# A Hyena, attention and PEER block on one core: 32 more tokens by gathering, five gather buffers, a rebuilt second normalization

## The chip, the cores and the metric

The kernel runs on one core of a Trainium2 chip. The metric is the device time of one execution in microseconds (us). Engines: TensorE (PE; PEld is its weight load), VectorE (DVE), ScalarE (ACT), GpSimd (POOL), SyncE (SP, which issues most transfers). TensorE's clock has two levels, 1.2 and 2.4 GHz; the mean granted clock of the profiled execution is 0.989 of the upper one.

## The reference, cut to what matters

512 tokens of 1024 numbers pass a token mixer (Hyena convolution and neighbourhood attention), then a PEER layer, which is what the change touches. Each token is normalized, and 8 heads pick 16 of 16384 experts each, so 128 picks a token. An expert is one row of U and one of V.

```python
def modulate(x, g, shift, scale):
    return rmsnorm(x, g) * (1.0 + scale) + shift
...
    q = (hf @ p['peer_w_q']).reshape(T, PEER_HEADS, 2, PEER_D_HALF)
    s = jnp.einsum('thpd,hpnd->thpn', q, p['peer_keys'])
    top_s, top_i = lax.top_k(s, PEER_TOPK)
    ...
    g = jax.nn.softmax(best_s, axis=-1)
        act = jax.nn.gelu(jnp.einsum('td,thkd->thk', xb, u_tab[ib]), approximate=False)
        return jnp.einsum('thk,thkd->td', gb * act, v_tab[ib])
        x_next = x_next + g2 * peer(modulate(x_next, p['norm2_g'], sh2, sc2), p)
```

## The kernel before

Products that need nearly full precision are made of halves: an operand is rounded to `h` (ScalarE, a copy into fp32r), the rest `l` is the difference (VectorE, sometimes GpSimd; `split`, line 205), and TensorE sums `h*h + h*l + l*h`.

The PEER layer treats the tokens in two ways. The first 128 take their rows by gathering: for each of the 128 picks, GpSimd issues an indirect transfer that brings one row of U (later of V) for each of 128 tokens into a tile `row` of 512 KB (line 1278, three buffers). VectorE makes the dot products with the normalized tokens `h2n` (line 1283), later the weighted sum of V rows (line 1292). This is the generator `sparse`, 256 steps, of which the calling loops take one or more at a time.

The other 384 tokens are dense. The 16384 experts are taken as 128 blocks i of 128. `low(i)` multiplies block i of U with the tokens: 24 matmuls of 384 columns (lines 233 and 235), whose gelu goes into a tile of the `ring` (51 buffers, line 1024). Which picks a token has is written as a dense matrix G: `spread` goes over 24 groups of 16 tokens, builds one-hot tiles on VectorE (`eq`, `gl`, `gh`, lines 1253 to 1258), multiplies them on TensorE (lines 1264 and 1265), evicts `st` on ScalarE and writes it to memory (`Gd`). G is read back for 8 blocks at a time (line 1076).

The V loop (line 1071) then does for each block i: `w` = ring * G on VectorE (line 1081); `wsh`, `wsl`, the halves of `w`; `vh`, `vl`, the halves of the block of V; and 18 matmuls of 512 columns into six accumulators, two for each 128 tokens (lines 223 to 225). As long as `low`s are left, one goes between two V products.

The stages in time: mixer to about 611 us; second normalization (`experts`, `modulate`, lines 423 to 435) with the two first query projections to 640; `route` (scores and top 16), with twelve `low`s between, to about 829; `columns` and `spread` with `low`s to 1028; V loop with 75 `low`s and then without them to 1891; the last output transfer ends the span.

The order on each engine is made by a scheduler when the program is built; the lines of code set its priorities, and `issue_after` holds an operation's transfers or gathers behind an instruction. Two buffers each hold `ws`, `v`, `wh`/`wl` (weight halves) and the PSUM tile of a `low`; three hold `raw` (weight blocks as loaded).

Of the kernel before, what the change touches and what calls it, by code (L numbers as in the profile page):

```python
# [34 lines left out]
NT = 3  # L35

RING = 51
# [132 lines left out]
class Kernel:  # L170
# [251 lines left out]
    def modulate(self, pool, h, xT, a, b, r, tap=None, bufs=2):  # L422
        nc = self.nc
        n = xT.shape[-1]
        for db in range(8):
            t = self.t(pool, "md", [128, n], bufs=bufs)
            nc.vector.tensor_tensor(t, r[db > 1] if isinstance(r, list) else r, xT[:, db, :], ALU.mult)
# [4 lines left out]
            last = self.split_into(h[0][:, db, :], h[1][:, db, :], t, "p" if db % 2 else "v")  # L432
            if tap is not None:
                tap(db, t)
        return last
# [357 lines left out]
    def run(self, st):  # L793
# [127 lines left out]
        with ExitStack() as s1:  # L921
# [38 lines left out]
            for tb in range(4):  # L960
# [10 lines left out]
                nc.sync.dma_start(xn[tb * 128:tb * 128 + 128, :], o)  # L971
            rb = self.t(self.pool(xst, "rb2", side="left"), "rb", [128, 512])
# [3 lines left out]
        self.sh2, self.a2 = sh2, a2  # L976
        self.experts(dr, [xst, yost, hst2, hst], x, xn, rb)
# [3 lines left out]
    def experts(self, dr, done, x, xn, r):  # L981

        nc, V = self.nc, self.nc.vector
        nd = NT * 128
# [4 lines left out]
        h2n = pl.tile([128, 1024], F32, name="h2n")  # L989
# [3 lines left out]
        with ExitStack() as s1:  # L993
            mp = self.pool(s1, "mod2", side="right")

            def tap(db, t):
                if db % 4 == 0:
                    nat.append(self.ps("s"))
                nc.tensor.transpose(nat[-1][:, (db % 4) * 128:(db % 4) * 128 + 128], t[:, 0:128], self.ident)
                if db % 4 == 3:  # L1000
                    nc.scalar.activation(h2n[:, (db - 3) * 128:(db + 1) * 128], nat[-1], AF.Copy)
            last = self.modulate(mp, h2, x, self.a2, self.sh2, r, tap, 4)
            with self.tc.issue_after(last[0]), self.tc.issue_after(last[1]):
                ks, row = self.tables(tp, mp)
# [30 lines left out]
        cols, rows, g0, mm = self.columns(cp, self.pool(s1, "picks", side="left"), pi, pj, pg, nd)  # L1035
# [4 lines left out]
        sparse = self.sparse(sp, h2n, rows, g0)  # L1040
# [9 lines left out]
        O = [[self.ps("s" if n < 4 else "t") for n in (2 * b, 2 * b + 1)] for b in range(NT)]  # L1050
# [10 lines left out]
        def finish(b, y, res):  # L1061

            o = self.t(sp, "row", [128, 1024], bufs=3)
            for hf in range(2):
                d = slice(hf * 512, hf * 512 + 512)
                V.tensor_tensor(o[:, d], y[hf], g2[:, d], ALU.mult)
                V.tensor_tensor(o[:, d], o[:, d], res[:, d], ALU.add)
            dst = self.A["out"].rearrange("(r q c) d -> q r c d", r=ROWS, q=QB)[b]
            nc.sync.dma_start(dst, o)

        for i in range(NE):
            while todo and todo[0] < i + RING:
                low(todo.pop(0))
            if i % 8 == 0:
                G = self.t(vp, "G", [128, nd // 16, 8, 16], bufs=2)
# [8 lines left out]
            if i < NE - 2:  # L1084
                products(i, range(NT))
            with self.tc.issue_after(ins):
                for _ in range((2 + i % 2) if todo else 1):
                    next(sparse, None)
            if i == NE - 8:
                g2 = self.load(self.wp, None, "wh", self.g2d, 2)  # L1090
                res = self.t(vp, "G", [128, 3, 1024], bufs=2)
                nc.sync.dma_start(res, xn[128:, :].rearrange("(b p) d -> p b d", p=128))
        r0 = self.t(self.wp, "wh", [128, 1024], F32, 2)
        nc.sync.dma_start(r0, xn[:128, :])
        for _ in sparse:
            pass
        finish(0, [self.acc[:, hf * 512:hf * 512 + 512] for hf in range(2)], r0)
        mm = products(NE - 2, [0])
        for b in range(3):
# [5 lines left out]
            finish(b + 1, O[b], res[:, b])  # L1105
        hs.close()

    def tables(self, tp, mp):
# [3 lines left out]
        row = self.load(tp, "sel", "row")  # L1112
        for g in range(4):
            s = slice(4 * g, 4 * g + 4)
            keys = self.load(mp, "keys", src=self.A["keys"][:, s], bufs=2)
            self.split_into(ks[0][:, s], ks[1][:, s], keys, "p" if g % 2 else "v")
        return ks, row

    def route(self, rp, h2, ks, row, pi, pj, pg, ahead):
# [3 lines left out]
        self.id16 = rp.tile([128, 128], F16, name="id16")  # L1123
        V.tensor_copy(self.id16, self.ident)
# [94 lines left out]
    def columns(self, cp, hp, pi, pj, pg, nd):  # L1219
# [3 lines left out]
        ei = cp.tile([128, 128], I32, name="ei")  # L1223
        V.scalar_tensor_tensor(ei, flat(pi), 128.0, flat(pj), op0=ALU.mult, op1=ALU.add)
        g0 = cp.tile([128, 128], F32, name="g0")
        V.tensor_copy(g0, flat(pg))
        hi = {}
        for n, x in (("i", pi), ("j", pj), ("g", pg)):
            p = self.ps("s", 128, nd)
            for b in range(NT):  # L1230
                mm = nc.tensor.transpose(p[:, b * 128:b * 128 + 128], x[:, 4 - NT + b].rearrange("p h k -> p (h k)"), self.ident).ins
            hi[n] = hp.tile([128, nd, 2], F16, name="p" + n)
            pp = p.unsqueeze(2).to_broadcast([128, nd, 2])
# [6 lines left out]
        return hi, ei, g0, mm  # L1240
# [29 lines left out]
    def sparse(self, vp, h2n, ei, g):  # L1270

        nc, V = self.nc, self.nc.vector
        dots = vp.tile([128, 128], F32, name="dots")
        acc = self.acc = h2n

        def gather(tab, n):
            r = self.t(vp, "row", [128, 1024], bufs=3)
# [3 lines left out]
        for n in range(128):  # L1281
            r = gather("u_rows", n)
# [27 lines left out]
```

## Time and profile before

| | us |
|---|---|
| median of 3 runs | 1901.79 (1900.74 to 1902.36) |
| profiled execution | 1902.87 |
| its span | 1901.1 |
| TensorE busy | 1817.8 (96%) |
| VectorE busy | 1470.5 (77%) |
| ScalarE busy | 836.3 (44%) |
| GpSimd busy | 566.9 (30%) |
| moved | 429.37 MB, mean 226 GB/s |

The busy share is a mean over stages with different limits. A stage's limit is seen in slices of the span, and within a slice in the timeline, where a row's bracket tells how long the engine sat idle ahead of it and who released it.

### The profile page before, as it was taken

What the parts mean: (1) busy time and instruction counts of PE and PEld (TensorE: products, weight loads), DVE (VectorE), ACT (ScalarE), POOL (GpSimd) and SP (SyncE); (2) the same over time, 40 slices, a digit from 0 to 9 for tenths busy, and PEclk for the clock granted to TensorE, in tenths of its full rate; (3) what the DMA queues carried; (4) which work ended last, traced back from release to release, by engine and by line L of the source; (5) the groups of instructions that cost most, each with busy time, mean ns of one, the idle gap of its engine ahead of it and who ended that gap; (6) DMA issues with size and microseconds to landing.
All of it is one profiled execution on the core that took longest, in us unless ns stands there. A gap on an engine that the chain in (4) does not pass through costs nothing.

```text
span 1901.1 us, 26935 instructions
## 1 busy us (share of the span) xinstructions
PE 1817.8 (96%) x9939; PEld 1566.5 (82%) x9939; DVE 1470.5 (77%) x2742; ACT 836.3 (44%) x1265; POOL 566.9 (30%) x381
## 2 busy tenths in 40 slices
PE   6999999999989899999999999999999999999997
PEld 1578887878867788899989898889999999988886
DVE  7879765656788788878997877778777777768875
ACT  2553434545552543346876333233333333333332
POOL 3440000000002433341221444444444444433410
PEclk9999999999999999999999999999999999999999
DMA  9453323333486322246888988889898888878873
GB/s 304 143 172 113 109 84 117 117 114 92 128 292 226 125 78 78 78 134 236 330 308 321 349 305 306 312 297 336 312 328 302 316 313 303 321 249 305 305 269 106
DMA packets 167389, 429.37 MB, mean 226 GB/s; under 512 B 14967, under 2 KB 70455, under 8 KB 163288
## 3 DMA queue, kind: packets, MB, share of 16 engines
q1 hardware_dynamic: 127112, 280.82, 43.9%
q0 software_dynamic: 40144, 146.82, 20.8%
q8 instruction: 78, 1.28, 0.3%
q14 instruction: 55, 0.45, 0.1%
HBM read 387.22 MB, written 38.27 MB: 224 GB/s over the span
## 4 chain that ended last, share of the span: by engine, by line
PE 73%; DVE 11%; issue 5%; POOL 3%; ACT 2%; DMA 1%; SPq 0%; ACTq 0%; DVEq 0%; POOLq 0%
PE a L233 26%; PE a L235 12%; PE s L223 7%; PE s L224 6%; PE s L225 6%; PE t L225 3%; PE t L224 3%; PE t L223 3%; POOL row L1278 3%; PE s L1264 1%; PE s L1265 1%; PE a L756 1%; DVE gh L1258 1%; DMA row<-in_u_rows,ei 1%; DVE sc L1155 1%
## 5 line engine op out<-in xcount | busy, mean ns | idle before, releaser
L233 PE MATMUL a<-h,wh 128*128 128x384 f32 (+1 forms) x2944 | 613.9, 358 | 6.2 <-ACT ring L1024 1.3
L233 PEld LDWEIGHTS a<-h,wh 128*128 128x128 f32 x2944 | 524.3, 189 | 53.8 <-DVE h L205 2.4
L204 ACT ACTIVATE wh<-raw 128x1024 fp32r<-128x1024 f32 (+1 forms) x208 | 213.7, 1027 | 358.5 <-DMA raw<-in_u_cols 162.9
L235 PE MATMUL a<-h,wl 128*128 128x384 f32 (+1 forms) x1472 | 318.4, 354 | 0.0
L1278 POOL DMA_INDIRECT row<-in_u_rows,ei x128 | 187.0, 1461 | 336.7 <-DVE row L1283 321.8
L1278 POOL DMA_INDIRECT row<-in_v_rows,ei x128 | 200.4, 1565 | 261.9 <-DVE h2n L1292 242.6
L235 PEld LDWEIGHTS a<-h,wl 128*128 128x128 f32 x1472 | 261.4, 188 | 17.4
L205 DVE TENSOR_TENSOR wl<-raw,wh 128x1024 fp32r<-128x1024 f32 (+1 forms) x173 | 203.8, 1178 | 60.5 <-ACT wh L204 40.0
L224 PE MATMUL s<-vl,wsh 128*128 128x512 f32 x512 | 200.0, 392 | 7.1 <-DVE vl L205 7.1
L1283 DVE SCALAR_TENSOR_TENSOR row<-row,h2n 128x1024 f32<-128x1024 f32 x128 | 155.0, 1220 | 57.0 <-DMA row<-in_u_rows,ei 56.8
L225 PE MATMUL s<-vh,wsl 128*128 128x512 f32 x512 | 198.3, 390 | 0.0
L204 ACT ACTIVATE wsh<-w 128x384 fp32r<-128x384 f32 x128 | 67.0, 524 | 287.8 <-PE t L224 137.9
L223 PE MATMUL s<-vh,wsh 128*128 128x512 f32 x512 | 176.2, 390 | 0.0
L1292 DVE SCALAR_TENSOR_TENSOR h2n<-row,dots,h2n 128x1024 f32<-128x1024 f32 x127 | 162.5, 1279 | 16.5 <-DMA row<-in_v_rows,ei 16.0
L205 DVE TENSOR_TENSOR vl<-raw,vh 128x1024 fp32r<-128x1024 f32 x128 | 155.8, 1218 | 5.9 <-ACT vh L204 5.8
L205 DVE TENSOR_TENSOR wsl<-w,wsh 128x384 fp32r<-128x384 f32 x128 | 71.1, 556 | 97.5 <-ACT wsh L204 81.9
L204 ACT ACTIVATE vh<-raw 128x1024 fp32r<-128x1024 f32 x128 | 134.5, 1051 | 26.1 <-DMA raw<-in_v_rows 23.3
L446 POOL DMA_DIRECT2D yv<-in_w_ada x32 | 17.2, 537 | 380.7 <-DVE yv L456 165.2
L205 POOL TENSOR_TENSOR wl<-raw,wh 128x1024 fp32r<-128x1024 f32 x35 | 85.0, 2428 | 125.4 <-PE a L235 106.8
L224 PEld LDWEIGHTS s<-vl,wsh 128*128 128x128 f32 x512 | 96.3, 188 | 26.8 <-DVE vl L205 9.8
L225 PEld LDWEIGHTS s<-vh,wsl 128*128 128x128 f32 x512 | 96.4, 188 | 19.9
L223 PEld LDWEIGHTS s<-vh,wsh 128*128 128x128 f32 x512 | 96.1, 188 | 17.5 <-ACT vh L204 0.5
(357 smaller groups left out, 2978.1 us busy)
## 6 DMA issues: line engine op xcount, KB each, us to landing
raw<-in_u_cols SPq DMA_DIRECT2D x128, 512.0 KB, 3.7
raw<-in_v_rows SPq DMA_DIRECT2D x128, 512.0 KB, 3.7
Gd<-st SPq DMA_DIRECT2D x24, 1024.0 KB, 5.3
G<-Gd SPq DMA_DIRECT2D x16, 1536.0 KB, 11.9
raw<-in_w_in SPq DMA_DIRECT2D x40, 512.0 KB, 3.9
yv<-in_w_ada POOLq DMA_DIRECT2D x32, 256.0 KB
adaw<-in_w_ada SPq DMA_DIRECT2D x16, 512.0 KB, 5.6
raw<-in_w_q SPq DMA_DIRECT2D x16, 512.0 KB, 3.4
```

Of the source, the lines that this page charges most:

```text
L204: return (nc.scalar.activation(hi, src, AF.Copy).ins, (nc.vector if eng == "v" else nc.gpsimd).tensor_tensor(lo, src, hi, ALU.subtract).ins)
L205: (nc.vector if eng == "v" else nc.gpsimd).tensor_tensor(lo, src, hi, ALU.subtract).ins)
L223: t.matmul(out, a[0], b[0], start=start, stop=False)
L224: t.matmul(out, a[0], b[1], start=False, stop=False)
L225: return t.matmul(out, a[1], b[0], start=False, stop=stop).ins
L233: t.matmul(out, w[0][:, c, :], h[x][:, c, :], start=(c == 0 and x == 0), stop=False)
L235: i = t.matmul(out, w[1][:, c, :], h[0][:, c, :], start=False, stop=(c == n - 1))
L756: nc.tensor.matmul(po[:, e], a, vv[:, tb, e], start=(n == 0), stop=False, skip_group_check=True)
L1155: V.match_replace(s, v[:, 0:8], s, -3.0e38)
L1278: nc.gpsimd.indirect_dma_start(out=r, out_offset=None, in_=self.A[tab], in_offset=bass.IndirectOffsetOnAxis(ap=ei[:, n:n + 1], axis=0))
L1283: V.scalar_tensor_tensor(r, r, 1.0, h2n, op0=ALU.mult, op1=ALU.mult, accum_out=dots[:, n:n + 1])
L1292: V.scalar_tensor_tensor(acc, r, dots[:, n:n + 1], acc, op0=ALU.mult, op1=ALU.add)
```

## The change

32 more tokens (`NX`) go by gathering. Their 128 picks are laid on 128 partitions as 4 groups of 32 picks by 32 tokens, so that a gather brings four picks of each of the 32 tokens: 32 gathers of U and 32 of V more, 320 steps in `sparse` instead of 256. Eight small transfers scatter the pick numbers and weights; the four partial sums are added at the end by two f32 matmuls of 512 columns with a selection matrix `sx`. 352 tokens stay dense (`ND`): a `low` has 24 matmuls of 352 columns, `spread` 22 groups; a V product still has 18 matmuls of 512 columns, for blocks of 128, 128 and 96 tokens. The gather buffers become five, the ring 47. A V iteration takes three steps of `sparse` while `low`s are left and then one or two in turn. Outputs and residuals are transferred in pieces where a block crosses a bound of the output's layout.

The second normalization is rebuilt: ScalarE scales x ahead by `a2` into a buffer (`gl[1]`, eight operations); a block then is one multiplication (VectorE), the high half with the shift as bias (ScalarE), the low half in one scalar_tensor_tensor (VectorE), and two narrow ScalarE copies `mu` for the transposes of the 128 and the 32 gathered tokens. GpSimd has no part in it. The four key blocks are loaded at its start, the cast of the identity moves from VectorE to ScalarE, and the late `w_ada` steps are taken three, two and one at a time.

```diff
+NX = 32
+ND = T - 128 - NX
+BL = [(b, min(128, ND - b)) for b in range(0, ND, 128)]
+ROWB = 5
-RING = 51
+RING = 47
...
-                    drain(late, 2)
+                    drain(late, 3 if ob < 2 else 2 if ob < 7 else 1)
...
+            for db in range(8):
+                nc.scalar.activation(gl[1][:, db, :], x[:, db, :], AF.Copy, scale=a2[:, db:db + 1])
...
-            last = self.modulate(mp, h2, x, self.a2, self.sh2, r, tap, 4)
+            keys = [self.load(mp, "keys", src=self.A["keys"][:, 4 * g:4 * g + 4], bufs=4) for g in range(4)]
+            for db in range(8):
+                t = self.t(mp, "md", [128, 512], bufs=3)
+                V.tensor_tensor(t, r[db > 1], x[:, db, :], ALU.mult)
+                hi = nc.scalar.activation(h2[0][:, db, :], t, AF.Identity, bias=self.sh2[:, db:db + 1]).ins
+                lo = V.scalar_tensor_tensor(h2[1][:, db, :], t, self.sh2[:, db:db + 1], h2[0][:, db, :], op0=ALU.add, op1=ALU.subtract).ins
+                u = self.t(mp, "mu", [128, 256])
+                for o, z in ((u[:, 0:128], t[:, 0:128]), (u[:, 128:256].rearrange("p (q t) -> p q t", t=NX), t[:, 128:128 + NX].unsqueeze(1).to_broadcast([128, 128 // NX, NX]))):
+                    nc.scalar.activation(o, z, AF.Identity, bias=self.sh2[:, db:db + 1])
+                tap(db, u)
...
-                    c, d = slice(b * 128, b * 128 + 128), slice(hf * 512, hf * 512 + 512)
-                    mm = self.mm3(O[b][hf], (ws[0][:, c], ws[1][:, c]), (v[0][:, d], v[1][:, d]), i == 0, i == NE - 1)
+                    c, d = slice(BL[b][0], sum(BL[b])), slice(hf * 512, hf * 512 + 512)
+                    mm = self.mm3(O[b][hf][:BL[b][1]], (ws[0][:, c], ws[1][:, c]), (v[0][:, d], v[1][:, d]), i == 0, i == NE - 1)
...
-                for _ in range((2 + i % 2) if todo else 1):
+                for _ in range(3 if todo else 1 + i % 2):
                     next(sparse, None)
...
+        finish(0, 128, [h2n[0][:, d] for d in halves], r0[0])
+        sx = sp.tile([128, NX], F32, name="sx")
+        V.tensor_reduce(sx, self.ident.rearrange("p (q t) -> p t q", t=NX), axis=AX.X, op=ALU.add)
+        y = [self.ps("a") for _ in halves]
+        for p, d in zip(y, halves):
+            nc.tensor.matmul(p[:NX], sx, h2n[1][:, d], start=True, stop=True)
+        finish(128, NX, [p[:NX] for p in y], r0[1])
...
+        for q in range(128 // NX):
+            nc.sync.dma_start(ei[1][q * NX:q * NX + NX], e1[:, q * NX:q * NX + NX])
+            nc.sync.dma_start(g0[1][q * NX:q * NX + NX], more[2][:, q * NX:q * NX + NX])
...
-            r = self.t(vp, "row", [128, 1024], bufs=3)
+            r = self.t(vp, "row", [128, 1024], bufs=ROWB)
```

The change also moves instructions. At the end of `spread`, ScalarE evicts the last group (`st`), then splits the first blocks of V (`vh`) and the first `w` (`wsh`); a `ring` there is the gelu of a `low` that TensorE has done in the meantime. Before:

```order
L1266 ACTIVATE st_10669<-s_10670 128x4x128
L1266 ACTIVATE st_10669<-s_10680 128x4x128
L1266 ACTIVATE st_10669<-s_10690 128x4x128
L1266 ACTIVATE st_10669<-s_10700 128x4x128
L204 ACTIVATE wh_10831<-raw_10829 128x1024
L1024 ACTIVATE ring_10742<-a_10717 128x384
L204 ACTIVATE vh_10795<-raw_10793 128x1024
L204 ACTIVATE vh_10864<-raw_10862 128x1024
L1024 ACTIVATE ring_10778<-a_10753 128x384
L204 ACTIVATE wh_10903<-raw_10901 128x1024
L204 ACTIVATE wsh_10801<-w_10799 128x384
```

and after:

```order
L1302 ACTIVATE st_10547<-s_10548 128x4x128
L1302 ACTIVATE st_10547<-s_10558 128x4x128
L1302 ACTIVATE st_10547<-s_10568 128x4x128
L1302 ACTIVATE st_10547<-s_10578 128x4x128
L210 ACTIVATE vh_10607<-raw_10605 128x1024
L210 ACTIVATE vh_10679<-raw_10677 128x1024
L210 ACTIVATE wsh_10613<-w_10611 128x352
```

Before, weights `wh` are still split and two `low`s end between the last eviction and the first `wsh`; after, none stands there. The ring is full sooner, so that behind the last one-hot product TensorE has one `low` (and three matmuls of another) ahead of the first V product where it had four.

In the V loop, ScalarE before has, behind each `wsh`, the halves of the next V and U blocks, and then the `ring` of a `low`:

```order
L1024 ACTIVATE ring_13547<-a_13522 128x384
L204 ACTIVATE wsh_13700<-w_13698 128x384
L204 ACTIVATE vh_13694<-raw_13692 128x1024
L204 ACTIVATE wh_13735<-raw_13733 128x1024
L1024 ACTIVATE ring_13619<-a_13594 128x384
L204 ACTIVATE wsh_13774<-w_13772 128x384
```

and after, at the place of about the 16th block:

```order
L210 ACTIVATE wsh_11695<-w_11693 128x352
L210 ACTIVATE vh_11617<-raw_11615 128x1024
L1041 ACTIVATE ring_11613<-a_11588 128x352
L210 ACTIVATE wsh_11769<-w_11767 128x352
L210 ACTIVATE wh_11656<-raw_11654 128x1024
L1041 ACTIVATE ring_11685<-a_11660 128x352
L210 ACTIVATE vh_11689<-raw_11687 128x1024
```

Here `wh_11656`, the weights of the `low` that follows on TensorE, has moved behind `wsh_11769`, and `vh_11689`, for the V product behind that `low`, stands behind the `ring` of that same `low` (`a_11660`). The first of these comes in seven iterations, the second in two.

VectorE in the V loop, before:

```order
L205 TENSOR_TENSOR wsl_13066<-w_13063,wsh_13065 128x384
L1081 TENSOR_TENSOR w_13132<-ring_9366,G_13055 128x384
L1283 SCALAR_TENSOR_TENSOR row_13156,dots<-row_13156,h2n 128x1024
L1283 SCALAR_TENSOR_TENSOR row_13159,dots<-row_13159,h2n 128x1024
L205 TENSOR_TENSOR vl_13060<-raw_13057,vh_13059 128x1024
L1283 SCALAR_TENSOR_TENSOR row_13162,dots<-row_13162,h2n 128x1024
L205 TENSOR_TENSOR wl_13096<-raw_13093,wh_13095 128x1024
L205 TENSOR_TENSOR wsl_13135<-w_13132,wsh_13134 128x384
```

and after:

```order
L211 TENSOR_TENSOR wsl_15314<-w_15311,wsh_15313 128x352
L1103 TENSOR_TENSOR w_15383<-ring_12047,G_15231 128x352
L1329 SCALAR_TENSOR_TENSOR h2n_6047<-row_15407,dots_8814,h2n_6047 128x1024
L1329 SCALAR_TENSOR_TENSOR h2n_6047<-row_15410,dots_8814,h2n_6047 128x1024
L211 TENSOR_TENSOR vl_15236<-raw_15233,vh_15235 128x1024
L1329 SCALAR_TENSOR_TENSOR h2n_6047<-row_15413,dots_8814,h2n_6047 128x1024
L211 TENSOR_TENSOR wl_15275<-raw_15272,wh_15274 128x1024
L211 TENSOR_TENSOR wsl_15386<-w_15383,wsh_15385 128x352
```

Before, `vl_13060` stands behind `wsl_13066`, its partner in the same V product. After, `vl_15236` stands behind `wsl_15314`, which belongs to the V product after its own (its partner is `wsl_15242`), and behind two gathered rows. In 49 of the iterations with `low`s it is so, in fifteen of them with two or more operations of 1024 columns ahead of `vl`; in these TensorE's order has the six products with `vh` ahead of the first with `vl`.

## Rows read from the trace of the kernel before

**Rows 1.** The page, engine totals: busy us (share of the span), instructions.

```profile
PE 1817.8 (96%) x9939; PEld 1566.5 (82%) x9939; DVE 1470.5 (77%) x2742; ACT 836.3 (44%) x1265; POOL 566.9 (30%) x381
```

**Rows 2.** Timeline of TensorE: start us, us, engine, line, operation, out<-in, count.

```profile
1405.30 0.40 PE L225 MATMUL t<-vh,wsl 128*128 128x512 f32 x1
1405.54 2.94 PE L233 MATMUL a<-h,wh 128*128 128x384 f32 x16
...
1409.70 0.39 PE L223 MATMUL s<-vh,wsh 128*128 128x512 f32 x1
...
1413.79 2.94 PE L233 MATMUL a<-h,wh 128*128 128x384 f32 x16
```

**Rows 3.** Timeline of TensorE at the first and the last V product.

```profile
1028.17 3.02 PE L233 MATMUL a<-h,wh 128*128 128x384 f32 x16
...
1044.90 0.39 PE L223 MATMUL s<-vh,wsh 128*128 128x512 f32 x1
...
1891.07 0.39 PE L225 MATMUL t<-vh,wsl 128*128 128x512 f32 x1
```

**Rows 4.** Waits of TensorE: engine line, waited for: us in total, times, longest.

```profile
PE s L224 <- DVE vl L205: 7.1, 6, 3.5
```

**Rows 5.** The page, groups: busy, mean ns, idle before, most of it released by.

```profile
L1278 POOL DMA_INDIRECT row<-in_u_rows,ei x128 | 187.0, 1461 | 336.7 <-DVE row L1283 321.8
...
L1283 DVE SCALAR_TENSOR_TENSOR row<-row,h2n 128x1024 f32<-128x1024 f32 x128 | 155.0, 1220 | 57.0 <-DMA row<-in_u_rows,ei 56.8
```

**Rows 6.** Slices: us, busy per engine PE, PEld, DVE, ACT, POOL, clock, DMA share, GB/s.

```profile
545.00:560.00 15.00, 12.58 (x53) 9.42 (x51) 14.79 (x25) 10.82 (x21) 0.00 (x0) 1.00 1.04 413
700.00:760.00 60.00, 56.12 (x336) 49.31 (x335) 50.40 (x269) 21.51 (x30) 20.26 (x10) 0.97 0.25 80
850.00:900.00 50.00, 50.00 (x374) 49.06 (x373) 42.01 (x43) 31.40 (x37) 8.41 (x5) 1.00 0.64 219
900.00:950.00 50.00, 47.78 (x444) 45.88 (x443) 50.00 (x52) 42.14 (x48) 11.76 (x7) 1.00 0.90 330
1310.00:1360.00 50.00, 50.00 (x256) 45.73 (x255) 38.99 (x57) 17.75 (x25) 23.41 (x17) 1.00 0.92 323
1735.00:1785.00 50.00, 50.00 (x223) 41.39 (x222) 41.83 (x50) 18.76 (x26) 21.04 (x13) 1.00 0.82 292
```

**Rows 7.** The tile gh on VectorE: ns min/median/max, first and last start, forms.

```profile
L1258 DVE TENSOR_TENSOR gh<-eqi,pg x21: 1209/1215/1220, 887.2 to 1024.9; 128x2048 f16<-128x2048 f16 x21
```

**Rows 8.** Timeline of all engines around the second normalization.

```profile
618.57 1.29 DVE L427 TENSOR_TENSOR md<-a,xnext 128x512 f32<-128x512 f32 x2 [1.37 <-ACT rb L973]
...
631.41 1.31 POOL L205 TENSOR_TENSOR h<-md,h 128x512 fp32r<-128x512 f32 x1 [1.55 <-ACT h L204]
...
638.85 1.28 DVE L1124 CAST id<-ident 128x128 f16<-128x128 f32 x1
...
639.82 0.33 PE L223 MATMUL t<-ks,qh 128*128 128x128 f32 x1 [1.93 <-ACT qh L204]
```

**Rows 9.** Timeline of ScalarE in the V loop.

```profile
1405.55 0.52 ACT L204 ACTIVATE wsh<-w 128x384 fp32r<-128x384 f32 x1 [3.11 <-issue]
1405.98 1.05 ACT L204 ACTIVATE vh<-raw 128x1024 fp32r<-128x1024 f32 x1
...
1409.90 0.49 ACT L1024 ACTIVATE ring<-a 128x384 f32<-128x384 f32 x1 [0.28 <-PE a L235]
```

**Rows 10.** Timeline of VectorE in the V loop.

```profile
1406.11 0.56 DVE L205 TENSOR_TENSOR wsl<-w,wsh 128x384 fp32r<-128x384 f32 x1 [1.13 <-ACT wsh L204]
1406.70 0.56 DVE L1081 TENSOR_TENSOR w<-ring,G 128x384 f32<-128x384 f32 x1
1407.59 1.28 DVE L1292 SCALAR_TENSOR_TENSOR h2n<-row,dots,h2n 128x1024 f32<-128x1024 f32 x1 [0.33 <-DMA row<-in_v_rows,ei]
1408.79 1.22 DVE L205 TENSOR_TENSOR vl<-raw,vh 128x1024 fp32r<-128x1024 f32 x1
```

**Rows 11.** Timeline of GpSimd in the V loop.

```profile
1400.47 1.68 POOL L1278 DMA_INDIRECT row<-in_v_rows,ei  x1 [2.34 <-DVE h2n L1292]
```

More of the change, by code (lines that the diff above doesn't have):

```diff
@@ L988, in experts @@
         h2 = [pl.tile([128, 8, 512], F32R, name=f"h2{i}") for i in range(2)]
-        h2n = pl.tile([128, 1024], F32, name="h2n")
+        h2n = [pl.tile([128, 1024], F32, name=f"h2n{i}") for i in range(2)]
         nat = []
@@ L997, in tap @@
                 if db % 4 == 0:
[L998 to L999 removed]
+                    nat[:] = self.ps("s"), self.ps("s")
+                for x, y in zip(nat, (t[:, 0:128], t[:, 128:256])):
+                    nc.tensor.transpose(x[:, (db % 4) * 128:(db % 4) * 128 + 128], y, self.ident)
                 if db % 4 == 3:
[L1001 to L1002 removed]
+                    for o, x in zip(h2n, nat):
+                        nc.scalar.activation(o[:, (db - 3) * 128:(db + 1) * 128], x, AF.Copy)
+            keys = [self.load(mp, "keys", src=self.A["keys"][:, 4 * g:4 * g + 4], bufs=4) for g in range(4)]
[8 more added lines that the diff above has]
+                tap(db, u)
+            last = hi, lo
             with self.tc.issue_after(last[0]), self.tc.issue_after(last[1]):
[L1004 removed]
+                ks, row = self.tables(tp, keys)
         for s in done:
@@ L1034, in experts @@
         s1 = ExitStack()
-        cols, rows, g0, mm = self.columns(cp, self.pool(s1, "picks", side="left"), pi, pj, pg, nd)
+        cols, rows, mm = self.columns(cp, self.pool(s1, "picks", side="left"), pi, pj, pg, nd)
         ts.close()
@@ L1039, in experts @@
         sp = self.pool(hs, "sparse", side="right")
-        sparse = self.sparse(sp, h2n, rows, g0)
+        sparse = self.sparse(sp, [(h, *r) for h, r in zip(h2n, rows)])
         with s1:
@@ L1049, in experts @@
         vp = self.pool(hs, "vphase", side="left")
-        O = [[self.ps("s" if n < 4 else "t") for n in (2 * b, 2 * b + 1)] for b in range(NT)]
+        O = [[self.ps("s" if n < 4 else "t") for n in (2 * b, 2 * b + 1)] for b in range(len(BL))]
         last = []
@@ L1056, in products, with finish @@
                 for hf in range(2):
-                    c, d = slice(b * 128, b * 128 + 128), slice(hf * 512, hf * 512 + 512)
-                    mm = self.mm3(O[b][hf], (ws[0][:, c], ws[1][:, c]), (v[0][:, d], v[1][:, d]), i == 0, i == NE - 1)
-            return mm
-        def finish(b, y, res):
-            o = self.t(sp, "row", [128, 1024], bufs=3)
+                    c, d = slice(BL[b][0], sum(BL[b])), slice(hf * 512, hf * 512 + 512)
+                    mm = self.mm3(O[b][hf][:BL[b][1]], (ws[0][:, c], ws[1][:, c]), (v[0][:, d], v[1][:, d]), i == 0, i == NE - 1)
+            return mm
+        def finish(n, m, y, res):
+            o = self.t(sp, "row", [128, 1024], bufs=ROWB)
             for hf in range(2):
                 d = slice(hf * 512, hf * 512 + 512)
[L1066 to L1069, printed above, removed]
+                V.tensor_tensor(o[:m, d], y[hf], g2[:m, d], ALU.mult)
+                V.tensor_tensor(o[:m, d], o[:m, d], res[:m, d], ALU.add)
+            dst = self.A["out"].rearrange("(r q c) d -> q r c d", r=ROWS, q=QB)
+            a = 0
+            while a < m:
+                q, r = divmod(n + a, 128)
+                k = min(128 - r, m - a)
+                nc.sync.dma_start(dst[q, r // 16:(r + k) // 16], o[a:a + k])
+                a += k
         for i in range(NE):
@@ L1084, in experts @@
             if i < NE - 2:
-                products(i, range(NT))
+                products(i, range(len(BL)))
             with self.tc.issue_after(ins):
-                for _ in range((2 + i % 2) if todo else 1):
+                for _ in range(3 if todo else 1 + i % 2):
                     next(sparse, None)
@@ L1104, in experts, with tables @@
                 mm = products(NE - 1, [b])
-            finish(b + 1, O[b], res[:, b])
+            finish(T - ND + BL[b][0], BL[b][1], [o[:BL[b][1]] for o in O[b]], res[:, b])
         hs.close()
-    def tables(self, tp, mp):
+    def tables(self, tp, keys):
         nc = self.nc
```

91 lines of the change are left out of this document (46 added, 45 removed).

## Prediction

> **What bounds the kernel now.** I read the engine totals first. TensorE is busy 1817.8 of 1901.1 us and VectorE 1470.5 [rows 1], so over the whole run the multiplications set the time; but a stage has its own limit, so I went on stage by stage.
>
> In the last and longest stage, the V loop, the row view of TensorE shows no gap between one product and the next [rows 2]. A `low` (the U product of one expert row) starts at 1405.54 and the next V product at 1409.70: 24 matmuls of 384 columns, 4.16 us. The next `low` starts at 1413.79: 18 matmuls of 512 columns, 4.08 us or 0.227 each. The loop runs from 1044.90 to 1891.46 (its last matmul starts at 1891.07) [rows 3]: 846.6 us. Of these, 128 x 4.08 = 522.2 are V products and 75 x 4.16 = 312.0 are the `low`s that are still to do. The other 12.4 are waits; 7.1 of them are for `vl` [rows 4], which stands behind gathered rows on VectorE, and VectorE in turn waits 57.0 us for U rows while GpSimd waits 321.8 for a row buffer [rows 5]. Three buffers are what makes the gathers late.
>
> Ahead of the loop, the 50 us slices show which engine is full [rows 6]: at 850 to 900 TensorE (50.00 of 50), at 900 to 950 VectorE (50.00), at 700 to 760 TensorE 56.12 of 60. The spread of G is thus VectorE's: its `gh` comes 21 times from 887.2 to 1024.9 [rows 7], 20 steps of 6.89 us.
>
> **The change part by part.** All sums are against the profiled execution (1902.87 us; span 1901.1), 1.1 above the median of the three runs.
>
> *Second normalization, -4 us (0 to -7).* Before, the chain is: first product of the block norms at 618.57, last low half on GpSimd ending at 631.41 + 1.31 = 632.72, two of the four key loads still to come, the cast of the identity at 638.85, the first scores at 639.82 [rows 8]. After, VectorE does two passes of about 0.64 a block (1.29 for two): 8 x 1.29 = 10.3 from 618.57, or 628.9, 3.8 sooner. ScalarE does one such pass and two of 128 columns a block and lies close behind; its eight extra pre-scalings fit only if they end before 618.57, which is the bound at 0. The keys and the cast no longer come last, which is worth up to 3 more.
>
> *Routing, -3 us (0 to -4).* Twelve `low`s stand here. A `low` of 352 columns is 352/384 of 4.16, 3.84 with the small fixed part: 0.31 less, 3.7 in all, if TensorE is the limit; at 56 of 60 it nearly is [rows 6].
>
> *Spread and start of the loop, -12.9 us (-10 to -15).* Two groups fewer in VectorE's stretch: 2 x 6.89 = 13.8. The eight `low`s of TensorE's stretch before it: 8 x 0.31 = 2.5. Against it, the order now has two `low`s ahead of the last group's one-hot products where there was one (less three matmuls that come behind): +3.4. From the last one-hot (the `low` behind it starts at 1028.17) to the first V product at 1044.90 are 16.7 us of eviction, the write of G, its read and `w`; before, four `low`s fill them. A ring of 47 instead of 51 leaves one there, so TensorE will stand idle for about 12.4 us. That idling isn't a cost of its own in this sum: what isn't done there is among the 79 `low`s that I count in the loop.
>
> *The V loop, -1 us (-12 to +25).* Work: 522.2, since its matmuls still have 512 columns (the last block's fewer rows save nothing) + 79 x 3.84 = 303.4, + 1 for the two extra f32 products and 1 for the start: 827.6. Waits come on top, laid down from the order and the rows at 1405. (a) In seven iterations ScalarE has the `wh` of the next `low` behind the `wsh` that waits for the V product's end: `wsh` starts 0.25 after the last V matmul's start, the next operation 0.43 later [rows 2, 9], and `wh` takes 1.05 like `vh`: the `low` starts 1.5 late, 7 x 1.5 = 10.5. (b) In two, `vh` stands behind the `ring` of the `low` just ended: 0.43 + 1.05 and the hand-over, 1.7 each, 3.4. (c) `vl`(i) now often stands behind `wsl`(i+1), as the order section shows; `wsl` starts 0.81 after the last V matmul's start, `w` 0.59 later [rows 10]; `w` then takes 0.44 (a little less than its row, for 352 columns), each gathered row some 1.17 (1.20 to the next start at 1407.59), `vl` 1.22. With two rows ahead it ends at 1.84 + 2 x 1.17 + 1.22 = 5.40 after that start. It is needed at 0.24 + 3.84 + 6 x 0.227 = 5.44, since the new order puts the six products with `vh` first in those iterations. So two rows just fit, with no slack; three (once, beyond those in (a) and (b)) cost 0.9. Sum of (a) to (c): 14.8. (d) Most of the 12.4 of before should go with five buffers: the gather issued at 1400.47 [rows 11] released its consumer at 1407.59 [rows 10], 7.1 us later; three buffers at 2.5 rows in 8.25 us give each 9.9 less its use, five at three rows in 7.92 us give 13.2. I keep 3 us for late ones, and let 0 and 12 stand as the ends. Total 827.6 + 14.8 + 3 = 845.4 against 846.6.
>
> In the stretch of V products alone, VectorE gets 1.5 rows instead of one per 4.08 us: `wsl` 0.55, `w` 0.44, `vl` 1.14, 1.5 x 1.20: 3.93 of 4.08, full but within. The 64 more gathers cost GpSimd some 1.5 us of issue each, where it waits for buffers now [rows 5]: nothing. The scattered picks, the extra residual and output transfers and the 32-row finish lie beside V products: nothing. The tail after the last matmul keeps its length.
>
> **Memory traffic** is what could break this. An iteration with a `low` will move two weight blocks, three gathered ones (0.524 MB each) and 0.18 of G: 2.80 MB in 7.92 us, 354 GB/s. One without: 0.524 + 0.786 + 0.18 = 1.49 MB in 4.08, 365. Before, the same stretches show 323 at a share of 0.92 and 292 at 0.82 [rows 6]. Taken up to a share of 1 that is 351 to 356; but at 545 to 560 the engines moved 413 at 1.04. I take the second for short stretches, and the first as the bound that gives the 3 us of (d) their upper end.
>
> The Trainium skill speaks against the change here: "DMA: Bandwidth & Descriptors", Specifications, puts the limit of one core's memory at about 358 GB/s. The trace disagrees for a short stretch (413 at 545 to 560), and no run here shows it over a long one. By that page only the V-only stretch would stretch, by an estimated 0.08 us in some 37 iterations, 3 us, and the forecast would be 1884.
>
> Sum: -4 - 3 - 12.9 - 1.2 = -21.1: 1881.8 for a run like the profiled one, 1880.7 against the median. **I forecast 1881 us.**
>
> **The rivals.** *Memory becomes the bound (slower).* Mixed traffic that ends at a rate R makes an iteration with a `low` 2.80/R long and one without 1.49/R. At 340 GB/s that is 8.24 and 4.38, against 8.10 (waits included) and 4.08: 81 x 0.14 + 37 x 0.30 = 22 us, all of the gain: 1903. At 330, 8.48 and 4.52: 31 + 16 = 47 us, 1928. It decides at about 341. For it: a share of 0.92 at 323. Against: 413 moved elsewhere. *VectorE is late for `vl`.* Some fifteen iterations have two or more wide operations between `wsl`(i+1) and `vl`(i) and no slack; another 26 have one and 1 us to spare. If each of the fifteen loses about 1 us to a late row or a slow hand-over, as the six waits of before did (7.1 us), the time is 1881 + 15 = 1896. For it: these waits are just of that kind. Against: more buffers. *More is won.* If ScalarE's order costs only half of (a) and (b), since the weights may be split early when TensorE is late anyway, and the normalization gives its 7: 1881 - 7 - 3 - 4 = 1867. *The buffers don't help:* gathers stay as late as before (10 instead of 3): 1888, within my band.
>
> **How the numbers follow.** Forecast with its band (1873 to 1889): 0.50. Memory: 0.18, of which 0.13 over 1906, 0.04 within, 0.01 below. `vl` late: 0.17 (1890 to 1902), of which 0.13 faster, 0.03 no change, 0.01 slower. More won: 0.15. About 0.2% (4 us) is what a measurement of this kernel can tell from no change. So faster 0.79, no change 0.07, slower 0.14. The range 1866 to 1902 leaves out the memory case's upper part and a little of the last.
>
> **What would show it.** The first V product near 1025 and the gap of 12 us before it; a `low` in 3.84 us; seven starts of a `low` late by 1.5 behind `wh`; waits for `vl` of a few us in all; a loop of 845 us; VectorE hardly waiting for gathered rows. I am wrong if iterations without `low` run over 4.2 us or rows are waited for throughout (memory), if `vl` costs more than 10 us (VectorE), or if the first scores don't come by 636.

## The result, and the profile after

The changed kernel takes 1932.91 us (median of 4 runs, 1928.77 to 1935.47) against 1902.07 (median of 4 runs of the kernel before beside them): a ratio of 1.0147, 95% interval 1.0126 to 1.0168. It is slower by 1.5%; 1881 was forecast, with a range of 1866 to 1902. The profiled execution has a span of 1931.4 us.

The page of the changed kernel, to be held against [rows 1] and [rows 5]: engine totals, then the groups of the `low`s, of the dot products and of the first V products (busy, mean ns, idle before and what ended most of it).

```profile
PE 1798.9 (93%) x9887; PEld 1512.8 (78%) x9887; DVE 1523.4 (79%) x2836; ACT 825.6 (43%) x1281; POOL 632.6 (33%) x441
...
L239 PE MATMUL a<-h,wh 128*128 128x352 f32 (+1 forms) x2944 | 592.0, 351 | 27.7 <-ACT wh L210 25.0
...
L1319 DVE SCALAR_TENSOR_TENSOR row<-row,h2n 128x1024 f32<-128x1024 f32 x160 | 191.3, 1216 | 1.2 <-issue 1.2
...
L229 PE MATMUL s<-vh,wsh 128*128 128x512 f32 x512 | 149.3, 402 | 23.3 <-ACT vh L210 12.7
```

TensorE is busy 18.9 us less than before and the run is 30 us longer, so it waits more. VectorE no longer waits for gathered rows (it idles 1.2 us ahead of the dot products, none of it for a row, against 57.0): the five buffers do what they were to do. But `low`s now wait 25.0 us for `wh`, ScalarE's half of a weight block, and V products 12.7 for `vh`. Before, no `low` and no V product of the V loop waited for these.

The waits of TensorE in the V loop while `low`s are left, and after (engine line, waited for: us in total, times, longest):

```profile
PE a L239 <- ACT wh L210: 25.0, 8, 8.4
PE s L229 <- ACT vh L210: 3.0, 2, 1.5
PE s L230 <- DVE vl L211: 0.9, 1, 0.9
```

```profile
PE s L229 <- ACT vh L210: 9.7, 3, 3.6
PE s L230 <- DVE vl L211: 1.0, 2, 0.5
```

The waits for `vl` of [rows 4] (7.1 us) have shrunk to 1.9. The place of the new waits is seen on the chain that ended last: among its longest pieces are now loads of weights, of which the chain before shows none (start us, us, what).

```profile
1060.95 17.36 DMA raw<-in_u_cols
...
1123.78 15.69 DMA raw<-in_u_cols
...
1196.04 19.21 DMA raw<-in_u_cols
...
1757.07 14.72 DMA raw<-in_v_rows
1795.28 14.20 DMA raw<-in_v_rows
1832.98 15.18 DMA raw<-in_v_rows
```

The chain has nine such loads of 512 KB, which take 11 to 19 us from their issue to their landing: four from 1060.95 to 1271.23, 63 to 75 us apart, one at 1666.07, and four behind it, 34 to 57 apart. G is read once in eight blocks, and each of the nine stands right behind such a read. (Behind the five reads from 1337 to 1598 TensorE never waits longer than 1.6 us.) The queue of SyncE around the longest of them, and ScalarE and TensorE there:

```profile
1190.60 0.33 SPq L1100 DMA_DIRECT2D raw<-in_v_rows  x1
1194.91 0.38 SPq L1098 DMA_DIRECT2D G<-Gd  x1
1196.04 9.43 SPq L222 DMA_DIRECT2D raw<-in_u_cols  x1
...
1217.62 0.33 SPq L1100 DMA_DIRECT2D raw<-in_v_rows  x1
```

```profile
1215.28 1.06 ACT L210 ACTIVATE wh<-raw 128x1024 fp32r<-128x1024 f32 x1 [6.97 <-DMA raw<-in_u_cols]
```

```profile
1216.38 4.66 PE L239 MATMUL a<-h,wh 128*128 128x352 f32 x16 [8.43 <-ACT wh L210]
...
1222.14 1.09 PE L229 MATMUL s<-vh,wsh 128*128 128x512 f32 x4
```

The read of G goes out at 1194.91. The load of the next U block stands directly behind it on SyncE and takes 9.43 us to be issued where a load takes 0.33 elsewhere; it lands at 1215.28, where ScalarE has waited 6.97 us for it; `wh` then lets the `low` start at 1216.38, after 8.43 us of idling. That `low` takes 5.8 us (to 1222.14) instead of 3.8. The reason for the longer `low` stands in the slices (columns as in [rows 6]; the clock is third from the right):

```profile
1160.00:1210.00 50.00, 47.95 (x253) 41.98 (x251) 42.07 (x64) 16.82 (x24) 24.91 (x19) 1.00 0.96 348
1210.00:1260.00 50.00, 43.62 (x222) 38.83 (x223) 37.08 (x56) 16.54 (x22) 22.85 (x17) 0.90 0.84 307
1212.00:1220.00 8.00, 3.62 (x12) 3.62 (x13) 3.63 (x5) 3.03 (x3) 1.00 (x1) 0.50 0.64 241
1222.00:1224.00 2.00, 2.00 (x11) 1.60 (x10) 2.00 (x4) 0.47 (x1) 1.39 (x2) 1.00 1.02 404
1735.00:1785.00 50.00, 46.12 (x192) 35.09 (x191) 42.69 (x51) 16.43 (x23) 23.09 (x16) 0.97 0.91 324
```

From 1212 to 1220, in the last 4 us of the idling and the first 4 behind it, the granted clock is 0.50, the lower of the two levels; from 1222 it is full again. So this stall cost about 2 us more than its wait. The traffic in the three long slices is 307 to 348 GB/s, where 354 and 365 were wanted, at a DMA share of 0.84 to 0.96. Read alone, this looks like the rival of the prediction, memory at its rate. It isn't, as the first experiment shows.

I took the loop apart by the distance from one V product's start to the next. The period is the commonest one; the excess is all that goes beyond it, summed over 123 of the 127 distances (the irregular ones at the loop's ends are left out).

| kernel | blocks with a `low`: period, excess | without: period, excess |
|---|---|---|
| before | 74 of 8.25, 10.0 us | 49 of 4.08, 0.0 |
| changed | 78 of 7.96, 41.1 | 45 of 4.14, 19.4 |
| changed, G reads on ScalarE's queue | 78 of 7.96, 18.0 | 45 of 4.14, 4.0 |
| changed, G in pieces | 78 of 7.96, 7.2 | 45 of 4.14, 3.1 |
| changed, one G read only | 78 of 7.96, -0.4 | 45 of 4.14, 2.2 |
| changed, three gather buffers | 78 of 7.97, 61.8 | 45 of 4.17, 16.4 |
| before, G in pieces | 74 of 8.25, 1.0 | 49 of 4.08, 0.0 |
| changed, without the added gathers | 78 of 7.96, 1.1 | 45 of 4.14, 2.1 |

The excess is more than the waits. In the changed kernel it is 60.5 us, of which the waits above are 39.6. Most of the rest is work at the lower clock: for the same matmuls TensorE is busy 855.83 us of the loop there, and 839.08 where G is read in pieces. The whole loop of either, changed first:

```profile
1022.10:1917.60 895.50, 855.83 (x4204) 725.36 (x4204) 726.82 (x915) 299.63 (x415) 413.49 (x293) 0.98 0.90 319
```

```profile
1024.10:1870.90 846.80, 839.08 (x4204) 713.12 (x4204) 722.28 (x915) 298.23 (x415) 398.47 (x293) 1.00 0.93 337
```

### The profile page after: what moved, and what is told of

Read it like the earlier page. It is cut to its first block, busy times and chain, and to the rows that moved or that the text cites. A ratio compares the mean times of both kernels' runs of the same rounds, so it can differ in the third digit from the quotient of the medians.

```text
span 1931.4 us, 27087 instructions
## 1 busy us (share of the span) xinstructions
PE 1798.9 (93%) x9887; PEld 1512.8 (78%) x9887; DVE 1523.4 (79%) x2836; ACT 825.6 (43%) x1281; POOL 632.6 (33%) x441
## 4 chain that ended last, share of the span: by engine, by line
PE 70%; DVE 12%; DMA 8%; ACT 3%; issue 2%; SPq 0%; POOL 0%; ACTq 0%; DVEq 0%; POOLq 0%
PE a L239 26%; PE a L241 12%; PE s L229 6%; PE s L230 6%; PE s L231 6%; DMA raw<-in_u_cols 4%; DMA raw<-in_v_rows 3%; PE t L229 3%; PE t L230 2%; PE t L231 2%; PE s L1300 1%; PE s L1301 1%; DVE gh L1294 1%; PE a L759 1%; ACT wh L210 1%
## 5 line engine op out<-in xcount | busy, mean ns | idle before, releaser
L239 PE MATMUL a<-h,wh 128*128 128x352 f32 (+1 forms) x2944 | 592.0, 351 | 27.7 <-ACT wh L210 25.0
L1313 POOL DMA_INDIRECT row<-in_u_rows,ei x160 | 226.7, 1417 | 324.0 <-DVE row L1319 290.0
L1313 POOL DMA_INDIRECT row<-in_v_rows,ei x160 | 231.9, 1449 | 229.2 <-DVE h2n L1329 208.8
L241 PE MATMUL a<-h,wl 128*128 128x352 f32 (+1 forms) x1472 | 306.4, 347 | 0.0
L210 ACT ACTIVATE wsh<-w 128x352 fp32r<-128x352 f32 x128 | 63.7, 498 | 335.2 <-PE t L230 209.2
L1329 DVE SCALAR_TENSOR_TENSOR h2n<-row,dots,h2n 128x1024 f32<-128x1024 f32 x158 | 202.3, 1280 | 1.2
L1319 DVE SCALAR_TENSOR_TENSOR row<-row,h2n 128x1024 f32<-128x1024 f32 x160 | 191.3, 1216 | 1.2 <-issue 1.2
L229 PE MATMUL s<-vh,wsh 128*128 128x512 f32 x512 | 149.3, 402 | 23.3 <-ACT vh L210 12.7
L1041 ACT ACTIVATE ring<-a 128x352 f32<-128x352 f32 x128 | 59.4, 464 | 206.0 <-PE a L241 205.2
L211 DVE TENSOR_TENSOR wsl<-w,wsh 128x352 fp32r<-128x352 f32 x128 | 66.8, 522 | 98.4 <-ACT wsh L210 94.8
```

The source lines that it names most:

```text
L210: return (nc.scalar.activation(hi, src, AF.Copy).ins, (nc.vector if eng == "v" else nc.gpsimd).tensor_tensor(lo, src, hi, ALU.subtract).ins)
L211: (nc.vector if eng == "v" else nc.gpsimd).tensor_tensor(lo, src, hi, ALU.subtract).ins)
L229: t.matmul(out, a[0], b[0], start=start, stop=False)
L239: t.matmul(out, w[0][:, c, :], h[x][:, c, :], start=(c == 0 and x == 0), stop=False)
L241: i = t.matmul(out, w[1][:, c, :], h[0][:, c, :], start=False, stop=(c == n - 1))
L1041: nc.scalar.activation(g, p, AF.Gelu)
```

## The experiments

My theory after the result: the **queue**. The weight loads stand in SyncE's queue behind a read of G of 1.4 MB in pieces of 512 bytes, and the added gathers make that read slow. Rivals: the **bytes** (the traffic as a whole is at its limit, the rival of the prediction), the **burst** (five gather buffers let gathers crowd out the loads), and, later, the **order** (the new order leaves no slack).

**G in eight pieces.** The read for the next eight blocks is cut by groups, and each piece is held behind the load of one V block (`vf`):

```diff
-                nc.sync.dma_start(G, Gd.rearrange("g j (i t) -> j g i t", t=16)[:, :, i:i + 8, :])
...
+            with self.tc.issue_after(vf):
+                e = i // 8 * 8 + 8
...
+                    a, b = (i % 8) * (nd // 16) // 8, (i % 8 + 1) * (nd // 16) // 8
+                    nc.sync.dma_start(Gn[:, a:b], Gd.rearrange("g j (i t) -> j g i t", t=16)[:, a:b, e:e + 8, :])
```

> The changed kernel with the read of G for the next 8 blocks cut into eight transfers of two or three groups, one behind each load of a V block; the bytes are the same. Queue theory: the weight loads are late because they stand behind a read of G of 1.4 MB in one piece; then the stalls of 2 to 9 us that come once in 8 iterations go, and the time is 1880 to 1892 us (V loop 845 to 855). Bytes theory: the traffic as a whole is at its limit; then the same waits come spread over all iterations, 1920 to 1935 us. Burst theory (five gather buffers crowd out the loads): little changes, 1915 to 1935.

Measured: 1886.94 us, 0.9929 of the kernel before (0.9907 to 0.9950). The excess falls from 41.1 to 7.2 and from 19.4 to 3.1 us. The waits in the loop and, below, two slices of this kernel:

```profile
PE a L239 <- ACT wh L210: 6.5, 8, 1.4
PE s L230 <- DVE vl L211: 1.2, 3, 0.5
```

```profile
1210.00:1260.00 50.00, 50.00 (x266) 44.16 (x265) 41.10 (x62) 18.32 (x26) 27.11 (x20) 1.00 1.01 374
1735.00:1785.00 50.00, 50.00 (x219) 38.82 (x218) 47.60 (x56) 17.62 (x25) 26.18 (x18) 1.00 1.02 370
```

The same bytes now move at 370 to 374 GB/s in these two slices, more than the 354 and 365 that the loop wants there and above the 341 at which the rival was to decide (from 1060 to 1810 the slices of 50 us show 329 to 374; the mean of the loop is 337 against 319). So the traffic was not at a limit where the loads came late: the bytes theory falls. The Trainium skill gives a limit of about 358 GB/s for one core ("DMA: Bandwidth & Descriptors", Specifications). The trace disagrees in these slices, with one core at work.

The order of instructions is another here than in the change, which is why this run alone does not tell the queue from the order.

**G read from ScalarE's queue.** One word of the read is changed, `nc.sync` to `nc.scalar`; in the V loop VectorE's and GpSimd's orders stay as in the change, ScalarE's but for one pair of operations, and TensorE's nearly.

> The changed kernel with the reads of G issued from ScalarE's queue instead of SyncE's, whole as before. Queue theory: the loads of weights no longer wait in SyncE's queue behind the read; the load issued next takes 0.4 us to issue instead of 4 to 9, and the time is 1890 to 1910 us, unless ScalarE itself is now held. Bytes theory: the loads share the same memory rate with the read and are as late as before: 1920 to 1935. Burst theory: 1920 to 1935.

Measured: 1898.22 us, 0.9991 of before (0.9976 to 1.0006). The loads are no longer held on SyncE: none of the loop takes longer than 0.38 us to be issued. (Below, a read of G in ScalarE's timeline and the load that follows it in SyncE's, then the waits of TensorE in the loop.)

```profile
1191.45 0.37 ACTq L1098 DMA_DIRECT2D G<-Gd  x1
1192.58 0.33 SPq L222 DMA_DIRECT2D raw<-in_u_cols  x1
```

```profile
PE a L239 <- ACT wh L210: 9.5, 7, 1.4
PE s L230 <- DVE vl L211: 3.5, 4, 1.4
PE s L229 <- ACT vh L210: 3.0, 2, 1.5
```

The excess is 18.0 + 4.0 us instead of 41.1 + 19.4. So of the 60.5 us, 38.5 are the place in the queue. What is left, 22.0, is near the 17.8 that the prediction laid down (14.8 from the order, and 3 for late rows), and the seven waits for `wh` (9.5 us, 10.5 were priced) and the two for `vh` (3.0, priced at 3.4) are those of its (a) and (b). This is the run that separates queue and order, since the order is kept.

**One read of G.** The reads after the first are left out; all blocks use the first eight blocks' part, so the output is another.

```diff
-            if i % 8 == 0:
+            if i == 0:
```

> The changed kernel with only the first of the 16 reads of G; all blocks then use the first 8 blocks' part, so 21.6 MB of reads are left out. Queue theory: no stall once in 8 iterations is left: 1872 to 1885 us. Bytes theory: demand falls from 354 to 331 GB/s (with a low) and from 365 to 321 (without): also 1875 to 1890. Burst theory: the stalls stay in part, above 1900.

Measured: 1873.23 us in one run, no stall once in eight blocks. This fits both queue and bytes; gathers and weight loads alone don't get in each other's way here. The scheduler also makes another order, in which TensorE never waits for `wh`, so the run doesn't tell queue from order either.

**Three gather buffers.** `ROWB = 3`.

> The changed kernel with three gather buffers instead of five. Burst theory: gathers are held back, the loads of weights are on time and the time falls below 1915 us. Queue and bytes theory: the weights are late at each read of G as before, and VectorE now also waits for rows, which the order of the change leaves no slack for: 1940 to 1980 us.

Measured: 1991.71 us, 1.0483 of before (1.0452 to 1.0514), longer than every theory had it.

```profile
PE s L230 <- DVE vl L211: 48.3, 33, 3.9
PE a L1127 <- DVE h2n L1329: 18.2, 1, 18.2
...
PE a L239 <- ACT wh L210: 3.0, 2, 1.6
```

The waits for `vl` (above, TensorE's) are back, 48.3 us where the kernel before had 7.1: with 320 gathers at this pace, five buffers are worth about 59 us (1991.71 - 1932.91). In the profiled runs, 57 us apart, 23 are in the loop and 33 behind the last V product, where the last gathered rows are waited for. The waits for `wh` fall to 3.0 us, which the queue theory did not say; TensorE comes later here, so the weights have more time. The holds on SyncE tell more than these waits. The load right behind a read of G takes 5.0 us to be issued on average here (the 14 reads in the loop), 4.9 with five buffers. So the number of buffers isn't what holds the loads, and the burst theory falls.

**Before, with G in pieces.** The same cut in the kernel before.

> The kernel before with G read in eight pieces, as a control. If the read in one piece also delays loads there: its waits of 12.4 us in the V loop go and it is 1890 to 1895 us. If those waits come from gathers with three buffers alone, and the loads had slack enough behind the read: 1899 to 1903.

Measured: 1900.00 us, 0.9980 of before (0.9958 to 1.0001): no difference that can be told, and inside the range of the theory that only the buffers matter. The traces say otherwise, but only in part. The excess in the loop falls from 10.0 to 1.0 us, and the loop (first V matmul to the end of the last) takes 837.7 us there, 846.6 before; VectorE waits for gathered rows as long as before (70.4 us against 72.8), so late rows alone don't make the waits for `vl`. But the scheduler makes another order here as well, and in the kernel with the second normalization alone (below), which also reads G in one piece, the loop takes 841.9. So the read in one piece cost the kernel before some 4 to 9 us of its loop in these profiled runs, and at least a part of what I had put down to too few gather buffers was this. That the time fell by only 2 lies at least in part in the profiled run's early part: the last output projection ended at 616.4 us there and at 610.9 in the profiled run of before, in stages that are the same in both.

**Without the added gathers.** The 64 gathers for the 32 tokens and their sums are left out (their part of the output is missing), the pace is that of before; G is read in one piece.

```diff
-        for (h, ei, g), s in zip(parts, dots):
+        for (h, ei, g), s in zip(parts[:1], dots):
...
-                for _ in range(3 if todo else 1 + i % 2):
+                for _ in range((2 + i % 2) if todo else 1):
```

> The changed kernel, G read in one piece as in the change, but without the 64 gathers of the 32 extra tokens (their sum is left out of the output), and with the pace of before: two or three gathers per block in turn, then one. Five buffers and the order of G reads stay. Load theory: a read of G in one piece is only too slow beside the added gathers; with the gathers of before, the load behind it is held 4 us instead of 4 to 9, TensorE's waits for weights in the V loop fall from 41 to below 12 us, 1870 to 1888 us. Order theory: the new order (a low's weights behind wsh, no slack behind the read) makes the stalls whatever the load; waits stay above 25 us and the time above 1900.

Measured: 1880.15 us in one run. The waits for weights in the loop are gone but for one:

```profile
PE a L239 <- ACT wh L210: 1.1, 1, 1.1
PE s L230 <- DVE vl L211: 0.5, 1, 0.5
```

Without the added gathers the read in one piece thus makes no stalls. The holds are shorter: the load right behind a read of G takes 2.8 us to be issued on average (14 reads in the loop), as in the kernel before (2.7), against 4.9 in the change. But load and order aren't separated by this run: the scheduler makes another order without the added gathers, and one load is still held 8.6 us on SyncE with no wait of TensorE behind it. How much of the gain is a shorter hold and how much is more slack stays open.

**The second normalization alone**, in the kernel before.

> The kernel before with the rebuilt second normalization alone (and the w_ada steps and keys as in the change). My step: the first scores come 2 to 4 us sooner and nothing behind takes it back: 1897 to 1900 us against 1902. Rival: VectorE's spread or the route swallows it: 1901 to 1903.

Measured: 1903.14 us, 0.9990 of before (0.9969 to 1.0012): no difference that can be told. In the traces, from the end of the last output projection's last row to the first scores (TensorE's timeline, here and in the changed kernel):

```profile
613.60 2.04 PE L235 MATMUL a<-m,wl 128*128 128x512 f32 x8
...
642.48 0.33 PE L223 MATMUL t<-ks,qh 128*128 128x128 f32 x1 [1.18 <-ACT qh L204]
```

```profile
610.14 2.04 PE L241 MATMUL a<-m,wl 128*128 128x512 f32 x8
...
637.69 0.31 PE L229 MATMUL t<-ks,qh 128*128 128x128 f32 x1
```

That is 26.84 us here and 25.51 in the changed kernel, against 28.95 before (608.84 + 2.03 to 639.82 in [rows 8]): 2.1 and 3.4 us won, where the prediction had 4. Such a gain is smaller than the scatter of the early stages: that last row ended at 615.64, 612.18 and 610.87 in the three profiled runs, with the same code ahead of it but for the pace of the `w_ada` steps.

**Aligned blocks**, together with G in pieces:

```diff
-BL = [(b, min(128, ND - b)) for b in range(0, ND, 128)]
+BL = [(0, 96), (96, 128), (224, 128)]
```

> The changed kernel with G read in pieces and the dense tokens in blocks of 96, 128 and 128 instead of 128, 128 and 96, so that each block ends on a bound of the output's layout and its output goes in one transfer. Tail theory: the span ends 13.8 us after the last matmul in the changed kernel against 9.6 before, because the split outputs move at about 50 to 150 GB/s instead of 170 to 215; then the tail is back at 9 to 10 us and the time is 1881 to 1885 against 1887 with pieces alone. Rival: the tail is set by the number of output bytes behind the last products; no change, 1886 to 1889.

Measured: **1882.50 us, 0.9887 of the kernel before (0.9856 to 0.9917)**, the fastest of the kernels whose output is complete; its interval overlaps that of pieces alone. From the last matmul to the end of the span it is 10.5 us, 14.2 with pieces alone, 13.8 in the changed kernel, 9.65 before. The last outputs go in three transfers as before, not five (SyncE's timeline, here and in the changed kernel):

```profile
1863.47 6.02 SPq L1090 DMA_DIRECT2D out<-row  x3
```

```profile
1914.17 6.13 SPq L1090 DMA_DIRECT2D out<-row  x5
```

**More ring, fewer gather buffers.** On top of these, `RING = 50` and `ROWB = 4`, which just fits; then the same with four gathers instead of three in each eighth block.

> As the one with pieces and aligned blocks, with 50 ring buffers and, for the room, four gather buffers instead of five. Three more lows stand behind the last one-hot product, in the 10.5 us that TensorE stands idle there, so 3 x 3.84 = 11.5 us of work leave the V loop: 1871 to 1876 if four gather buffers are enough; if they are not, VectorE waits for rows again, as with three buffers (1992), and it is 1885 to 1930.

> As the one with 50 ring and four gather buffers, with four instead of three gathers in each eighth block, so that the last rows aren't left for the end (where VectorE kept TensorE waiting 18.7 us). If the pace was the cause: 1868 to 1878 us. If four buffers can't bring the rows sooner whatever the pace: 1885 to 1900.

Measured: 1895.25 us, 0.9953 of before (0.9934 to 0.9972), and 1891.47 in one run. Both lose what they win, at the end (waits of TensorE in the second, from 1000 on):

```profile
PE a L1136 <- DVE h2n L1338: 18.6, 1, 18.6
PE s L229 <- ACT vh L210: 1.4, 1, 1.4
```

The wait at the start is gone (2.5 us for `wsh` are left in the first, 0.2 in the second) and the loop has no long stall, but the products with `sx` wait 18.6 us for the last gathered rows (18.7 in the first). The other pace didn't change that, so the pace in one block of eight wasn't the cause; whether four buffers are, or where the scheduler puts the last rows, wasn't tried.

## Why the prediction was wrong

The start of the loop came out near the forecast. The first V product and the wait ahead of it:

```profile
1010.15 1.43 PE L241 MATMUL a<-h,wl 128*128 128x352 f32 x8
1022.10 0.80 PE L229 MATMUL s<-vh,wsh 128*128 128x512 f32 x1 [10.52 <-ACT wsh L210]
```

1022.10 where 1025.0 was forecast (1044.90 in [rows 3]), and an idle time of 10.52 where 12.4 was. Part of this nearness is luck, as the terms were off both ways. The first scores came 2.1 us sooner than before, not 4, and later than the 636 that was named as a sign of being wrong. From there to the last search of the top 16 (MATCH_REPLACE8, started at 816.31 against 825.87) 7.4 us were won, not 3. From that to the first V product it was 13.2, against 12.9. In the loop a `low` takes 3.8 us, as said (it is the product of a block of 128 experts, not of one row). The waits for `vl` stayed small, and the seven late starts of a `low` behind `wh` are seen alone where G is read by ScalarE's queue (9.5 us). Three rows ahead of `vl` would have cost 1.1 by the prediction's own numbers, not 0.9, which changes nothing.

**The step that failed is the V loop**, forecast at 845.4 us. It ran from 1022.10 to 1917.59, 895.5 us, 50.1 more:

- Waits and what follows them: an excess of 60.5 us instead of 17.8 (14.8 from the order and 3 for late rows), 42.7 of the 50.1. Of the 60.5, 39.6 are waits, and most of the rest is work at the lower clock behind them, which the prediction put at nothing. Of the whole, 38.5 go when the read of G leaves SyncE's queue. The term "(d)" of the sum priced late gathers alone, and the part on memory traffic priced a mean rate. Neither asked in which queue the read of G stands and which load stands next. I had laid down where the changed order leaves weights and `vl` no slack, and didn't ask of each transfer how late it may come; the weight loads, with three buffers and one read of G ahead of them, were the ones that mattered. The row for it was to be had: in the kernel before, a load behind a read of G was held too, by up to 5.77 us (SyncE's timeline there):

```profile
1078.94 0.38 SPq L1076 DMA_DIRECT2D G<-Gd  x1
1082.32 5.77 SPq L1078 DMA_DIRECT2D raw<-in_v_rows  x1
1089.00 0.33 SPq L216 DMA_DIRECT2D raw<-in_u_cols  x1
```

- The V product: 4.14 us instead of 4.08, some 7 us over the loop. "Its matmuls still have 512 columns" was right, and yet they stand 0.230 apart on average instead of 0.227. In the kernel with aligned blocks products of 4.18 and 4.08 take turns. Why was not tried; that cause stays open.

The tail was held to keep its length and grew by 4.2 us (13.85 against 9.65). The prediction put the extra output transfers at nothing, as lying beside V products, and overlooked that five output transfers go out at the very end (1914.17 to 1920.30), the last of them behind the last product. Aligned blocks gave back 3.7 (14.2 with pieces alone, 10.5 with both).

So: 1880.0 for the span forecast, -2.9 for the start, +50.1 for the loop, +4.2 for the tail: 1931.4, the span measured. With pieces and aligned blocks the time is 1882.5, near the forecast, but not term by term, since the order is another there. The fairer test is the read by ScalarE's queue, which keeps the order: its loop takes 857.6 us, 12.2 above the forecast, of which some 7 are the V product and 4.2 the excess. So the queue was by far the largest missing term, and the V product and the tail were smaller ones.

**The rivals.** "Memory becomes the bound" got 0.18 and named the right side. Its mechanism is refuted: with the same bytes, G in pieces, the loop takes 846.9 us (1024.03 to 1870.90). "The buffers don't help" is wrong: rows are hardly waited for. "`vl` late" didn't come.

**The argument for five buffers** was right in effect (with three, the changed kernel takes 59 us more) and partly wrong in its reason: I read the waits of before as late gathers for want of buffers; with G in pieces and three buffers the excess fell from 10.0 to 1.0, in one profiled run and another order.

## What to carry to other kernels

Before adding traffic to a loop, list for each queue what stands directly behind its largest transfer, and how late that may land; a mean rate below the limit says nothing on it. A periodic large read should be cut into pieces that go out one by one behind the loads they would otherwise hold, or go by another queue. Where a scheduler sets the order, an operation's slack has to be counted anew after each change, for transfers as well as engines.

## What the runs showed of the hardware

- A load of 512 KB, issued on SyncE right behind a read of 1.4 MB in packets of 512 bytes, occupied its engine for up to 9.43 us, at most 0.38 when that read went out by ScalarE's queue, and at most 0.96 when it was cut into eight. The next issue on SyncE came only behind it (1205.56, behind 1196.04 + 9.43): the engine is held, not only the transfer.
- That hold grew with the gathers, and not with their buffers: 2.7 and 2.8 us on average with 256 gathers (the kernel before, whose reads are of 1.5 MB, and the change without the added ones), 4.9 and 5.0 with 320 (five buffers and three).
- One core moved 370 to 374 GB/s of gathers, loads and G reads over single slices of 50 us (G in pieces).
- In a stall of 8.43 us the granted clock fell to the lower level, and TensorE ran at it for some 4 us behind the stall: a `low` took 5.8 us instead of 3.8.
- The last outputs moved more slowly in five transfers than in three: 96 GB/s over the last 13 us of the changed kernel, 143 over the last 10 of the one before (slices of each, the rate at the right). Whether the number of transfers does it, or that the last block has 96 rows instead of 128, wasn't separated: aligned blocks change both.

```profile
1918.00:1931.00 13.00, 0.00 (x0) 0.00 (x0) 1.51 (x3) 0.00 (x0) 0.00 (x0) 0.58 0.26 96
```

```profile
1891.00:1901.00 10.00, 0.46 (x3) 0.03 (x1) 2.38 (x4) 0.00 (x0) 0.00 (x0) 0.69 0.41 143
```
